# All low weight parts on VectorE, and other counts of filler products, in a two-layer mixer and MoE kernel

## The chip, the cores and the metric

One core of a Trainium2 chip runs the whole program. The time is device time of one execution in microseconds (us), and a kernel is given by the median of its runs. TensorE (PE in the rows) multiplies, VectorE (DVE), ScalarE (ACT) and GpSimd (POOL) work on vectors, SyncE (SP) issues the loads of the weights.

## What is computed

The reference is a decoder of two layers over 256 tokens of width 1024, all in float32:

```python
for layer in range(DEPTH):                                    # DEPTH = 2
    mix = token_mixers(h, ...)        # y = h @ w_in; three head groups; concat @ w_out
    h = layer_norm(DN_ALPHA * h + mix, ...)
    ffn = moe_ffn(h, ...)             # 16 experts of width 512, the router picks two of a token
    h = layer_norm(DN_ALPHA * h + ffn, ...)
```

In `token_mixers` the product `h @ w_in` is cut into columns for three groups. Group A is gated linear attention ("G" below), group B is causal softmax attention over the one block of 256 tokens ("M"). Group C ("S") is softmax attention over 64 keys that an indexer picks for each query: a score of every earlier key, and then the top 64 of each row. The three results side by side are multiplied by `w_out`.

## The kernel before

**Products.** The mixer's weights are used in two parts. `Pieces.fill` (L586) takes a piece of a weight tile `wf` that a load has brought in, lets ScalarE copy it to a rounded high part `whi` and subtracts to get the low part `wlo`; the activations are split alike (`hhi`, `hlo`). A projection then adds three products for every piece and token tile: `pj<-whi,hhi`, `pj<-whi,hlo` and `pj<-wlo,hhi`. `Pieces.next` makes some pieces ahead of their use (four in the projections, three in the output projection). Which engine subtracts is decided by the number of the piece:

```python
(pool if self.i % SHARE == SHARE - 1 and self.i >= FROM else eng).tensor_sub(lo, src, hi.bitcast(F32))
```

With SHARE 5 and FROM 24 that is GpSimd for 13 of a layer's 88 pieces. Two more are made on GpSimd at the border of the layers, by another call.

**The order of the work.** A planner, class `Order` (L78), writes one list of instructions for each engine. It keeps a clock for each engine from its own costs. A backbone makes the seven projections in the order I, V, GV, M, S, GK, GG and then the output projection. Around it run tasks (indexer, attention, linear attention), and each goes on when what it waits for is due by the planner's clock of PE. So a change of a planned cost, or of the engine of an instruction, moves the places at which the tasks' products stand between those of the backbone. In the indexer each of the eight rounds of the top-k search waits for the planner's DVE clock:

```python
for _ in range(8):
    yield lambda: od.clk["DVE"] <= od.clk["PE"] + 400
    dve.max(out=m8, in_=acc)
    dve.match_replace(out=acc, in_to_replace=m8, in_values=acc, imm_value=SENT)
```

**Attention S.** `softmax_pv` (L613) goes over two query tiles, t = 0 with 128 keys and t = 1 with 256. PE multiplies (`sc<-qkT`), DVE adds the mask of the picked keys and takes the row maxima (`s_sb,mx<-sc,acc`, four heads), ACT takes the exponentials (`s_sb<-s_sb,mx`), DVE divides (`ri`, then `s_sb<-s_sb,ri`), PE transposes (`pT<-ident,s_sb`) and multiplies by the values (`pv<-pT,v`), and ACT and DVE split the result into two `mx` tiles, called `mixS`. Group A ends in a like chain: PE `o<-W,X`, ACT squares (`sq<-o`), DVE sums them (`ms<-sq`), GpSimd takes the root (`ms<-ms,mhalf`), DVE scales and gates (`og<-o,ms`, `og<-og,sg`), PE transposes (`tr<-ident,og`), and this becomes `mixG`.

**Output projection.** It uses its eight row blocks in the order `OUT_ORDER = (4, 6, 2, 0)`, two at a time. The first two (4, 5) take group B's result, the next two (6, 7) take `mixS`, and before these the backbone waits (`yield mixS`, L1164); the last four take `mixG`. Each pair of blocks is eight groups of three products (`po<-whi,mx` x2, `po<-wlo,mx`).

**Filler.** `warm(n, w)` issues products whose result nobody reads: at the start on a tile of ones, while the first weights are loaded, and in some pauses on the identity. In the router (`choose`, L1296) the picks of each token tile (`hot`) are counted with a product `pos<-hot,strict`, DVE makes positions and selection matrices `G` from it, and PE gathers the expert's tokens with them (`xT<-G,h`).

Of the kernel before, what the change touches and what calls it, by code (L numbers as in the profile page):

```python
# [9 lines left out]
F32 = mybir.dt.float32  # L10
# [34 lines left out]
N_T4 = 9  # L45
N_SM = 10
N_WS = 4
SHARE = 5
FROM = 24
N_WO = 3  # L50
N_UNITS = ((1, 3), (2, 6))
N_WARM0 = 7
N_AHEAD = 5
LAG = 350.0
TRIG = 5487.999999999999
N_FILL = 2
N_LAST = 2
N_WARM = 2
N_LEAD = 7
N_WARM2 = 4  # L60
TWO = (1, 3, 5)
AGAIN = {(0, 'g', 5), (1, 'g', 2), (1, 'g', 0), (1, 'd', 1), (1, 'd', 6), (1, 'd', 4), (2, 'g', 3), (2, 'd', 6)}
FILL = (1, 2)
# [180 lines left out]
def trunk_kernel(ctx, tc, x, positions, w_in, gate_up, gate_bias, norm_gain, w_out, ln_mix_g, ln_mix_b,  # L244
# [8 lines left out]
    pe, act, dve, pool = od.pe, od.act, od.dve, od.pool  # L253
# [4 lines left out]
    def bank(name="ps"):  # L258
        b = pp.tile([P, 512], F32, name=name, tag="ps")
        od.take(b.tensor.name)  # L260
        return b

    def t2(name, shape=(P, 512), dt=F32):
        return wp.tile(list(shape), dt, name=name, tag="t2", bufs=N_T2)
# [80 lines left out]
    def more(n=1):  # L345
        for _ in range(n):
            while issued[0] < len(specs) and specs[issued[0]][0] in extra:
                issued[0] += 1
            if issued[0] >= len(specs):
                return  # L350
            key, (parts, nk, w) = specs[issued[0]]
            issued[0] += 1
            t = fp.tile([P, nk, w], F32, name="wf", tag="wf")
            for at, src in parts:
                nc.sync.dma_start(t[:, at[0], at[1]] if at else t.rearrange("p k n -> p (k n)"), src)
            feed[key] = t
# [66 lines left out]
    ident = cp.tile([P, P], F32, name="ident")  # L423
# [77 lines left out]
    def mm(o, a, b, start=True, stop=True):  # L501
        pe.matmul(o, a, b, start=start, stop=stop, skip_group_check=True)
# [59 lines left out]
    def warm(n, w):  # L562

        b_ = bank("warm")
        for i in range(2 * n):
            mm(b_[:, 0:P], w, ones)
        od.free(b_)

# [8 lines left out]
    class Pieces:  # L577
# [8 lines left out]
        def fill(self, eng=dve):  # L586
            while self.i < len(self.plan) and self.i < self.j + self.ahead:
                key, kk, c0, n = self.plan[self.i]
                src = feed[key][:, kk, c0:c0 + n]
                hi = t2("whi", (P, n), F32R)  # L590
                lo = t2("wlo", (P, n), F32R)
                act.activation(hi, src, AF.Copy)
                (pool if self.i % SHARE == SHARE - 1 and self.i >= FROM else eng).tensor_sub(lo, src, hi.bitcast(F32))
                units[key] = feed[key]
                self.made[self.i] = hi, lo
                self.left[key] -= 1
                if not self.left[key]:
                    feed.pop(key)
                    more()
                self.i += 1  # L600
# [72 lines left out]
    def weight_pieces(l):  # L673
        plan = []
        for key in ORDER:
            _, groups, cols = CHUNKS[key]
            for i, nk in enumerate(groups):
                plan += [((l, key, i), kk, cols[0] * j, n) for kk in range(nk) for j, n in enumerate(cols)]
        for k0 in OUT_ORDER:
            plan += [((l, "O", k0 + kk), 0, 512 * n, 512) for kk in range(2) for n in range(2)]  # L680
        return Pieces(plan, N_WS)
# [75 lines left out]

    units, begun = {}, set()
    warm(N_WARM0, ones)
    pieces = weight_pieces(0)  # L760
    hhi, hlo = halves(0)
# [4 lines left out]
    for l in range(DEPTH):  # L766
# [529 lines left out]
        def choose(t):  # L1296

            s, g = slice(t * E, t * E + E), slice(4 * t, 4 * t + 4)
            top1, top2 = (top[:, i:i + 1] for i in (2 * t, 2 * t + 1))
            x4 = sel[:, s].rearrange("p (g e) -> p g e", e=4)  # L1300
            xa, xj = (x4[:, :, :, None].to_broadcast([P, 4, 4, 4]), x4[:, :, None, :].to_broadcast([P, 4, 4, 4]))
            rank4 = rank[:, s].rearrange("p (g e) -> p g e", e=4)
            yield dve.tensor_add(sel[:, s], sc[:, s], rb)
            dve.tensor_add(sums[:, g, 0:2], x4[:, :, 0:2], x4[:, :, 2:4])
            dve.tensor_add(sums[:, g, 2:4], x4[:, :, 0::2], x4[:, :, 1::2])
            rev = bass.AP(tensor=sel.tensor, offset=sel.offset + t * E + 3, ap=[sel.ap[0], [4, 4], [-1, 2]])
            yield dve.tensor_add(sums[:, g, 4:6], x4[:, :, 0:2], rev)
            dve.tensor_reduce(gs[:, g], sums[:, g], AX.X, OP.max)
            yield dve.tensor_tensor(gt[:, g], xj, xa, op=OP.is_gt)
            dve.tensor_reduce(top1, gs[:, g], AX.X, OP.max)  # L1310
            yield dve.tensor_tensor(ge[:, g], xj, xa, op=OP.is_ge)
            dve.scalar_tensor_tensor(at[:, g], gs[:, g], top1, pref[:, 0:4], op0=OP.is_equal, op1=OP.mult)
            yield dve.copy_predicated(gt[:, g], below[:, None].to_broadcast([P, 4, 4, 4]), ge[:, g])
            dve.tensor_reduce(top2, at[:, g], AX.X, OP.max)
            yield dve.tensor_reduce(rank4, gt[:, g], AX.X, OP.add)
            yield dve.tensor_scalar(at[:, g], at[:, g], top2, None, op0=OP.is_ge)
            yield dve.scalar_tensor_tensor(hot[:, s].rearrange("p (g e) -> p g e", e=4), rank4, 1.5,
                                           at[:, g, None].to_broadcast([P, 4, 4]), op0=OP.is_lt, op1=OP.mult)
            if t == 0:
                mm(pc[:, 0:E], strict, hot[:, 0:E])  # L1320
            else:
                mm(pc[:, E:2 * E], strict, hot[:, E:2 * E])
            yield dve.tensor_scalar(pos[:, s], hot[:, s], -1000.0, 1000.0, op0=OP.mult, op1=OP.add)
            yield dve.tensor_add(pos[:, s], pos[:, s], pc[:, s])
# [159 lines left out]

        pc = bank("pos")
        steps = [choose(t) for t in range(NT)]
        for _ in range(N_LEAD):
            next(steps[0])
        score(1)
        dve.tensor_scalar(mvs[1][:, 4:5], mvs[1][:, 0:1], mvs[1][:, 3:4], -1.0, op0=OP.mult, op1=OP.mult)  # L1490
        act.activation(h[1], h[1], AF.Identity, scale=mvs[1][:, 3:4], bias=mvs[1][:, 4:5])
        warm(N_WARM, ident)
        for _ in steps[0]:
            next(steps[1])
# [68 lines left out]
        for p in range(E // 2):  # L1563
# [54 lines left out]
            for i in range(8):  # L1618
                n, k = (i // 4, i % 4) if p >= FIN - 1 else (i % 2, i // 2)
# [39 lines left out]
        if last:  # L1659
            finish(z, sb, sts, *vecs[2:])  # L1660
            break
        warm(N_WARM2, ident)

        def close(t, z, st, hhi, hlo, nxt=l + 1, sb=sb, g2=vecs[2], b2=vecs[3]):
# [56 lines left out]
```

## Time and profile before

| | before |
|---|---|
| median of 3 runs (lowest, highest) | 717.87 us (717.22, 718.0) |
| the profiled execution, its span | 717.56 us, 715.5 us |
| PE busy | 687.1 us, 96% |
| DVE busy | 443.9 us, 62% |
| ACT busy | 273.6 us, 38% |
| POOL busy | 75.0 us, 10% |
| mean granted clock of TensorE | 0.993 |
| HBM traffic, mean | 341 GB/s |

The span reaches from the first to the last instruction. The profiled execution is 2.06 us longer than its span, and lies within the three timed runs. Busy shares are means over stages that differ: a mixer of about 150 us and an expert stage of about 200 us in each layer.

### The profile page before, as it was taken

To read this page: it belongs to the slowest core of one execution; us is meant where nothing else is said; L and a number is where in the kernel's file an instruction comes from. 1 tells how busy PE (TensorE), PEld (TensorE's weight loads), DVE (VectorE), ACT (ScalarE), POOL (GpSimd) and SP (SyncE) were. 2 spreads that over 40 slices of the span, in tenths; PEclk is the share of its full clock that TensorE was granted. 3 is DMA by queue.
4 is the path that set the end of the run, shared out by engine and by line. 5 is a ranking of instruction groups with operands and counts; after the bars stand their busy time and mean duration, and the time that the engine had idled before them with its cause. 6 is when DMAs were issued, how large, how long until landed. Compare 5 with 4: busy or idle time off the path is not lost. (4 is left out here: it accounts for less than half of the span.)

```text
span 715.5 us, 11300 instructions
## 1 busy us (share of the span) xinstructions
PE 687.1 (96%) x3885; PEld 399.2 (56%) x3885; DVE 443.9 (62%) x1091; ACT 273.6 (38%) x579; POOL 75.0 (10%) x102
## 2 busy tenths in 40 slices
PE   9999999999999989999899999999999999899993
PEld 8887878843533533533487879787435334343330
DVE  6778887652445454767487787867243556259646
ACT  5578675431212201212276676564223022022121
POOL 2021022200000001200121111121000000021002
PEclk9999999999999999999999999999999999999997
DMA  9799937979999999999999844479899999999971
GB/s 306 272 388 407 408 120 250 325 293 408 409 403 408 407 407 408 408 410 407 334 391 401 313 154 146 132 251 338 323 408 408 403 407 409 407 407 409 409 288 59
DMA packets 83533, 244.05 MB, mean 341 GB/s; under 512 B 10180, under 2 KB 14344, under 8 KB 83464
## 3 DMA queue, kind: packets, MB, share of 16 engines
q1 hardware_dynamic: 82792, 242.91, 89.0%
q8 instruction: 34, 0.56, 0.3%
q10 hardware_dynamic: 416, 0.26, 0.1%
q14 instruction: 35, 0.29, 0.1%
q0 software_dynamic: 256, 0.03, 0.0%
HBM read 242.13 MB, written 1.05 MB: 340 GB/s over the span
## 5 line engine op out<-in xcount | busy, mean ns | idle before, releaser
L239 PE MATMUL gu<-wf,xT 128*64 128x512 f32 x912 | 226.0, 594 | 3.6 <-PEq L1437 3.6
L239 DVE SCALAR_TENSOR_TENSOR yt<-y,ws,yt 32x512 fp32r<-32x512 f32 (+1 forms) x116 | 86.7, 748 | 94.9 <-ACT yt L239 93.4
L239 PEld LDWEIGHTS gu<-wf,xT 128*64 128x64 f32 x912 | 71.8, 137 | 131.7 <-issue 123.3
L239 DVE TENSOR_TENSOR wlo<-wf,whi 128x512 fp32r<-128x512 f32 (+3 forms) x148 | 89.6, 640 | 39.5 <-ACT whi L239 28.5
L239 PE MATMUL y<-wf,actT 128*64 128x512 f32 x432 | 110.5, 595 | 1.8 <-ACT actT L239 1.8
L239 ACT ACTIVATE whi<-wf 128x512 fp32r<-128x512 f32 (+3 forms) x176 | 86.1, 553 | 9.8 <-PE po L239 3.6
L239 PE MATMUL pj<-whi,hhi 128*128 128x512 f32 (+2 forms) x224 | 77.4, 356 | 0.4 <-ACT whi L239 0.4
L239 ACT ACTIVATE yt<-y,ws 128x512 fp32r<-128x512 f32 x60 | 36.8, 687 | 104.5 <-PE y L239 94.9
L239 PE MATMUL pj<-whi,hlo 128*128 128x512 f32 (+2 forms) x224 | 75.4, 347 | 0.0
L239 PEld LDWEIGHTS y<-wf,actT 128*64 128x64 f32 x432 | 34.0, 137 | 54.1 <-issue 42.0
L239 DVE TENSOR_TENSOR act<-act,gu 128x512 f32<-128x512 f32 x16 | 11.0, 688 | 83.7 <-PE gu L239 77.1
L239 PE MATMUL pj<-wlo,hhi 128*128 128x512 f32 (+2 forms) x224 | 60.5, 356 | 0.4 <-DVE wlo L239 0.4
L239 POOL TENSOR_TENSOR wlo<-wf,whi 128x512 fp32r<-128x512 f32 (+3 forms) x28 | 32.4, 1158 | 220.1 <-ACT whi L239 183.6
L239 PE MATMUL gu<-wx,xT 128*64 128x512 f32 x112 | 52.7, 596 | 0.0
L239 PEld LDWEIGHTS pj<-whi,hhi 128*128 128x128 f32 x224 | 42.1, 188 | 7.3 <-issue 1.7
L239 PEld LDWEIGHTS pj<-whi,hlo 128*128 128x128 f32 x224 | 42.1, 188 | 4.7
L239 ACT ACTIVATE actT<-aT 128x512 f32<-128x512 f32 x16 | 9.5, 594 | 85.4 <-PE aT L239 85.4
L239 PEld LDWEIGHTS pj<-wlo,hhi 128*128 128x128 f32 x224 | 37.5, 188 | 6.6 <-issue 1.2
L239 ACT ACTIVATE xT<-xT,cols 128x256 f32<-128x256 f32 x32 | 17.4, 564 | 57.2 <-PE xT L239 57.2
L239 ACT ACTIVATE act<-gu 128x512 f32<-128x512 f32 x16 | 9.6, 597 | 75.9 <-PE gu L239 75.9
L239 PE MATMUL y<-wx,actT 128*64 128x512 f32 x80 | 33.4, 595 | 0.0
L239 DVE TENSOR_TENSOR z<-z,sc 128x512 f32<-128x512 f32 x48 | 29.7, 680 | 0.4 <-PE sc L239 0.4
(268 smaller groups left out, 948.1 us busy)
## 6 DMA issues: line engine op xcount, KB each, us to landing
wf<-in_w_expert_gate_dram SPq DMA_DIRECT2D x114, 512.0 KB, 10.2
wf<-in_w_expert_up_dram SPq DMA_DIRECT2D x114, 512.0 KB, 10.1
wf<-in_w_expert_down_dram SPq DMA_DIRECT2D x108, 512.0 KB, 10.0
wf<-in_w_in_dram SPq DMA_DIRECT2D x32, 512.0 KB, 9.8
wx<-in_w_expert_down_dram SPq DMA_DIRECT2D x36, 256.0 KB, 5.9
wf<-in_w_out_dram SPq DMA_DIRECT2D x16, 512.0 KB, 11.1
wx<-in_w_expert_up_dram SPq DMA_DIRECT2D x24, 256.0 KB, 6.9
wx<-in_w_expert_gate_dram SPq DMA_DIRECT2D x10, 512.0 KB, 10.1
```

Of the source, the lines that this page charges most:

```text
L239: return fn(*a, **kw)
```

## The change

All low parts that the mixer's `fill` hands out by number go to VectorE. `warm(n, w)` now issues n products where it issued 2n; two of its calls, which issued 4 and 8 products, still do, and the one at the start issues 11 where it issued 14. In `choose` two products on the identity follow the first `pos<-hot,strict`.

```diff
--- before.py
+++ after.py
@@ -45,19 +45,18 @@
 N_T4 = 9
 N_SM = 10
 N_WS = 4
-SHARE = 5
-FROM = 24
 N_WO = 3
 N_UNITS = ((1, 3), (2, 6))
-N_WARM0 = 7
+N_WARM0 = 11
+N_KEEP = 2
 N_AHEAD = 5
 LAG = 350.0
 TRIG = 5487.999999999999
 N_FILL = 2
 N_LAST = 2
-N_WARM = 2
+N_WARM = 4
 N_LEAD = 7
-N_WARM2 = 4
+N_WARM2 = 8
 TWO = (1, 3, 5)
 AGAIN = {(0, 'g', 5), (1, 'g', 2), (1, 'g', 0), (1, 'd', 1), (1, 'd', 6), (1, 'd', 4), (2, 'g', 3), (2, 'd', 6)}
 FILL = (1, 2)
@@ -562,7 +561,7 @@
     def warm(n, w):
 
         b_ = bank("warm")
-        for i in range(2 * n):
+        for i in range(n):
             mm(b_[:, 0:P], w, ones)
         od.free(b_)
 
@@ -590,7 +589,7 @@
                 hi = t2("whi", (P, n), F32R)
                 lo = t2("wlo", (P, n), F32R)
                 act.activation(hi, src, AF.Copy)
-                (pool if self.i % SHARE == SHARE - 1 and self.i >= FROM else eng).tensor_sub(lo, src, hi.bitcast(F32))
+                eng.tensor_sub(lo, src, hi.bitcast(F32))
                 units[key] = feed[key]
                 self.made[self.i] = hi, lo
                 self.left[key] -= 1
@@ -1318,6 +1317,7 @@
                                            at[:, g, None].to_broadcast([P, 4, 4]), op0=OP.is_lt, op1=OP.mult)
             if t == 0:
                 mm(pc[:, 0:E], strict, hot[:, 0:E])
+                warm(N_KEEP, ident)
             else:
                 mm(pc[:, E:2 * E], strict, hot[:, E:2 * E])
             yield dve.tensor_scalar(pos[:, s], hot[:, s], -1000.0, 1000.0, op0=OP.mult, op1=OP.add)
```

The first place that moves is attention S of t = 1 in layer 0, on PE; layer 1 moves alike. Before, the stretch of the GG projection in which its second half stands reads as below; its `sc<-qkT 128x256 x4` stands sixteen rows higher, in the same projection, and `o<-W,X` belongs to group A.

```order
L239 MATMUL o<-W,X 64x128 x8
L239 MATMUL pj<-whi,hhi 128x512
L239 MATMUL pj<-whi,hlo 128x512
L239 MATMUL pj<-whi,hhi 128x512
L239 MATMUL pj<-whi,hlo 128x512
L239 MATMUL pj<-wlo,hhi 128x512 x2
L239 MATMUL pT<-ident,s_sb 128x128 x8
L239 MATMUL pv<-pT,v 64x128 x12
```

After, the same steps stand in the output projection. Four groups of `po` stand ahead of these rows, and behind them come `tr<-ident,og 128x128 x8` and then the first `po` that uses `mixS`:

```order
L238 MATMUL sc<-qkT 128x256 x4
L238 MATMUL o<-W,X 64x128 x8
L238 MATMUL po<-whi,mx 128x512 x2
L238 MATMUL po<-wlo,mx 128x512
L238 MATMUL po<-whi,mx 128x512 x2
L238 MATMUL po<-wlo,mx 128x512
L238 MATMUL po<-whi,mx 128x512 x2
L238 MATMUL po<-wlo,mx 128x512
L238 MATMUL po<-whi,mx 128x512 x2
L238 MATMUL po<-wlo,mx 128x512
L238 MATMUL pT<-ident,s_sb 128x128 x8
L238 MATMUL pv<-pT,v 64x128 x12
```

So the scores, the transposes and the product with the values have moved from among the products of GG to between the first eight groups of the output projection, and only four groups are left between `sc` and `pT`; all `tr<-ident,og` of group A now stand behind `pv` and ahead of the other `po`.

The second place is DVE, from the last row maximum of these four heads to the division. Before:

```order
L239 ISA s_sb,mx<-sc,acc 128x256
L239 ISA mx 128x1
L239 TENSOR_SCALAR mx<-mx 128x4
L239 TENSOR_TENSOR wlo<-wf,whi 128x512
L239 SCALAR_TENSOR_TENSOR W<-W,eb,kv 64x128 x4
L239 TENSOR_TENSOR wlo<-wf,whi 128x512
L239 RECIPROCAL ri<-mx 128x4
L239 TENSOR_SCALAR s_sb<-s_sb,ri 128x256 x4
L239 SCALAR_TENSOR_TENSOR W<-W,eb,kv 64x128 x4
```

After:

```order
L238 ISA s_sb,mx<-sc,acc 128x256
L238 ISA mx 128x1
L238 TENSOR_SCALAR mx<-mx 128x4
L238 TENSOR_TENSOR wlo<-wf,whi 128x512 x2
L238 RECIPROCAL ri<-mx 128x4
L238 TENSOR_SCALAR s_sb<-s_sb,ri 128x256 x4
L238 TENSOR_REDUCE ms<-sq 128x4
L238 TENSOR_SCALAR ms<-ms 128x4
L238 TENSOR_TENSOR og<-o,ms 128x512
L238 TENSOR_TENSOR og<-og,sg 128x512 x2
```

Two `wlo` stand between the maxima and the division in both, the second of them in wait for a `whi`; after the change the whole tail of group A (`ms`, `og`) stands behind the division.

The third place is ACT around the exponentials of these heads. Before:

```order
L239 ACTIVATE s_sb,mx<-s_sb,mx 128x256 x4
L239 ACTIVATE whi<-wf 128x512 x2
L239 ACTIVATE sq<-o 128x512
L239 ACTIVATE pT<-pT 128x512 x2
L239 ACTIVATE whi<-wf 128x512
L239 ACTIVATE mx<-pv 128x512
L239 ACTIVATE sq<-o 128x512
```

After:

```order
L238 ACTIVATE whi<-wf 128x512 x2
L238 ACT_TABLE_LOAD
L238 ACTIVATE s_sb,mx<-s_sb,mx 128x256 x4
L238 ACTIVATE sq<-o 128x512
L238 ACTIVATE whi<-wf 128x512
L238 ACTIVATE pT<-pT 128x512 x2
L238 ACTIVATE mx<-pv 128x512
```

Ahead of the exponentials a load of the function table has come in, since the two `sg` of GG now run before them; behind them a squaring and one `whi` stand before the copies of the transposed tiles.

## Rows read from the trace of the kernel before

**Rows 1.** Page, parts 1 and 2: busy us of each engine; HBM traffic by slice.
```profile
PE 687.1 (96%) x3885; PEld 399.2 (56%) x3885; DVE 443.9 (62%) x1091; ACT 273.6 (38%) x579; POOL 75.0 (10%) x102
...
GB/s 306 272 388 407 408 120 250 325 293 408 409 403 408 407 407 408 408 410 407 334 391 401 313 154 146 132 251 338 323 408 408 403 407 409 407 407 409 409 288 59
```

**Rows 2.** Timeline, 101 to 115 us, layer 0: start, length, engine, operation, [wait].
```profile
101.75 1.13 PE L239 MATMUL sc<-qkT 64*128 64x256 f32 x8
...
104.43 0.63 DVE L239 TENSOR_SCALAR mx<-mx 128x4 f32<-128x4 f32 x1
...
105.10 0.51 ACT L239 ACTIVATE s_sb<-s_sb,mx 128x256 f32<-128x256 f32 x1
...
107.09 1.13 ACT L239 ACTIVATE whi<-wf 128x512 fp32r<-128x512 f32 x2
...
107.73 0.69 DVE L239 TENSOR_TENSOR wlo<-wf,whi 128x512 fp32r<-128x512 f32 x1 [0.92 <-ACT whi L239]
...
108.40 1.09 PE L239 MATMUL o<-W,X 128*64 128x128 f32 x16
...
108.55 1.15 DVE L239 TENSOR_SCALAR s_sb<-s_sb,ri 128x256 f32<-128x256 f32 x4
...
110.92 1.03 PE L239 MATMUL pT<-ident,s_sb 128*128 128x128 f32 x8
...
111.89 1.58 PE L239 MATMUL pv<-pT,v 128*64 128x128 f32 x24
112.34 0.17 DVE L239 TENSOR_SCALAR ms<-ms 128x4 f32<-128x4 f32 x1
...
112.59 1.05 POOL L239 TENSOR_TENSOR ms<-ms,mhalf 128x4 f32<-128x4 f32 x1 [7.55 <-DVE ms L239]
...
114.74 0.68 DVE L239 TENSOR_TENSOR og<-o,ms 128x512 f32<-128x512 f32 x1
```

**Rows 3.** Timeline, 117 to 123 us, layer 0, output projection.
```profile
117.11 1.28 ACT L239 ACT_TABLE_LOAD   x1
...
117.51 0.62 PE L239 MATMUL po<-whi,mx 128*128 128x512 f32 x2
...
122.28 0.61 PE L239 MATMUL po<-whi,mx 128*128 128x512 f32 x2
```

**Rows 4.** Page, part 5: the low parts made on GpSimd.
```profile
L239 POOL TENSOR_TENSOR wlo<-wf,whi 128x512 fp32r<-128x512 f32 (+3 forms) x28 | 32.4, 1158 | 220.1 <-ACT whi L239 183.6
```

**Rows 5.** Timeline, 68.9 to 70.5 us, layer 0.
```profile
68.97 1.28 POOL L239 TENSOR_TENSOR wlo<-wf,whi 128x512 fp32r<-128x512 f32 x1 [6.45 <-ACT whi L239]
69.09 1.31 DVE L239 TENSOR_TENSOR y<-rope 128x128 f32<-128x128 f32 x1
...
70.46 0.66 PE L239 MATMUL tr<-ident,y 128*128 128x128 f32 x4 [0.75 <-DVE y L239]
```

**Rows 6.** Timeline, 414 to 417 us, layer 1.
```profile
414.15 1.63 POOL L239 TENSOR_TENSOR wlo<-wf,whi 128x512 fp32r<-128x512 f32 x1 [6.07 <-ACT whi L239]
...
417.07 0.57 PE L239 MATMUL bT<-mc,la 128*128 128x128 f32 x3 [0.59 <-DVE la L239]
```

**Rows 7.** Windows of the `warm` products alone: stretch, length, PE busy (records), ...
```profile
3.00:5.00 2.00, 2.00 (x11) 2.00 (x11) 0.00 (x0) 1.00 0.80 171
...
6.25:6.75 0.50, 0.50 (x6) 0.49 (x4) 0.00 (x0) 1.00 1.05 411
```

**Rows 8.** Timeline, 5 to 7 us: the first weight piece and the first projection.
```profile
5.50 0.78 ACT L239 ACTIVATE whi<-wf 128x292 fp32r<-128x292 f32 x2 [2.94 <-DMA wf<-in_w_in_dram]
...
6.76 1.15 PE L239 MATMUL pj<-wf,hT 128*128 128x292 f32 x4
```

**Rows 9.** Timeline, router of layer 0.
```profile
147.24 1.18 PE L239 MATMUL xT<-G,h 128*128 128x128 f32 x8 [1.08 <-DVE top L239]
```

**Rows 10.** Timeline, PE alone, around 258 us: a wait in the expert stage.
```profile
258.19 1.08 PE L239 MATMUL gu<-wf,xT 128*64 128x512 f32 x4 [1.80 <-PEq L1437]
```

**Rows 11.** Windows, end of the span: PE, PEld, DVE, ACT, POOL busy; granted clock; DMA.
```profile
706.00:707.00 1.00, 0.00 (x0) 0.00 (x0) 0.96 (x4) 0.48 (x1) 0.55 (x2) 0.51 0.00 0
```

## The prediction

> **What bounds the kernel now.** The page comes first. PE is busy for 96% of the span, and no other engine is above 62% [rows 1]. The row of HBM traffic shows some 408 GB/s through the expert stages, and 120 to 340 in slices 6 to 9 and 23 to 29, where the later parts of the mixers lie [rows 1]. There neither DVE nor the memory is at its limit, so time is lost or won only where a product on PE waits for another engine, and a microsecond that PE loses in a mixer moves all that comes after. I therefore read the timeline of the mixers, looking for PE rows with a wait, and for the steps that the change puts elsewhere.
>
> **The change part by part.**
>
> *Attention S moves into the output projection.* This carries the sum. Before, its second tile (t = 1) lies in the GG projection, and from the start of `sc` at 101.75 to the start of `pT` at 110.92 PE has other products to do; its `pT` row shows no wait at all [rows 2]. After, the listing of PE leaves between `sc` and `pT` only `o<-W,X` and four groups of `po`. I price both sides from one origin, T = start of `sc`.
>
> PE's side: `sc` 1.13, `o<-W,X` 1.09 [rows 2]; seven groups of `po` lie between 117.51 and 122.28, that is 0.68 each, four make 2.73 [rows 3]. PE is through at about T+4.9.
>
> The chain's side, with the lengths that the same steps have before [rows 2]: the exponentials start at T+3.35 (105.10) and end at T+5.34 (107.09, where ACT goes on). Behind them ACT now does `sq` and one `whi`, 0.57 each (1.13 for two), until T+6.5. DVE's second `wlo` waits for that `whi`; from its start to the start of the division there were 0.82 (107.73 to 108.55), so the division starts at T+7.4, a quarter of its 1.15 is one head, and the first transposes can start at T+7.7. PE has then waited **2.8**. The last head is divided at T+8.5, so the eight transposes, which take 0.97 by themselves (110.92 to 111.89), end at T+8.8, and `pv` ends at T+10.3, 1.5 later. Meanwhile the tail of group A stands behind the division on DVE: the sum of squares, priced as the other DVE pass over 512 columns at 0.68, the scaling with its hop to GpSimd 0.25 (112.34 to 112.59), GpSimd's root 1.05, `og<-o,ms` 0.68, and the first gating another 0.68: T+8.5 plus 3.35 makes T+11.85. `tr<-ident,og` stands ahead of every further `po`, so PE waits again from T+10.3, **1.55**, and some 0.3 more for the last transposed heads and for the second half of `og`. That is 4.65. Against it the exponentials may start up to 0.45 sooner, since the scaling of the maxima took 0.63 before (104.43), and a DVE operation of the same form (112.34) 0.17. I take **4.5 us per layer, 9.0 in all**. Bounds: 3.2, if the `sq`, `whi` and `wlo` ahead of the division (0.57, 0.57 and 0.69, some 1.3 of which then falls away) find room while the scores are made; 5.7, if DVE comes to the maxima late by one wait for GpSimd's root (1.05), which now lies in the same stretch.
>
> The other edit there, one more load of a function table on ACT ahead of the exponentials, is 1.28 [rows 3]. From the end of GG ACT has two `sg`, one `pT`, two `whi` at some 0.57 each and this load, 4.1 in all, while PE does four groups (2.7) and four transposes (some 0.5) and the maxima come 3.35 after that, at 6.5. So I cost it at nothing; with that cover gone it would be 1.28 per layer. The four transposes of t = 0 come after two groups of `po`, and I cost them at nothing too, between 0 and 1.
>
> *Low parts on DVE.* GpSimd loses 26 of its 28 pieces of 1.16 [rows 4], and DVE gets 26 at 0.69 [rows 2], 18 us over both mixers. PE uses a piece in six products, two groups or 1.36, and pieces are made four ahead, so 0.69 of DVE for each is covered. What the trace shows of the other direction: beside a GpSimd piece that ran from 68.97 for 1.28, a DVE operation on 128 columns took 1.31, more than the 0.68 of one on 512, and PE waited 0.75 for it [rows 5]. In layer 1 a piece from 414.15 for 1.63 lies ahead of a wait of 0.59 [rows 6]. These two waits should go: **-1.35**, between -0.6 (one of them is refilled by the added subtractions) and -2.0 (with small ones of 0.2 elsewhere).
>
> *The start.* Three products fewer are six records. They come at about 0.2 each early on, and at 0.1 or a little less in the last half microsecond [rows 7]. The first projection starts at 6.76, right behind the filler, although its weights were there by 5.50, when ACT began to round them [rows 8]. It could start 1.0 sooner. It then lies in part in the stretch in which products still take twice as long, which gives back some 0.25, and later weights have to be there as well. I take **-0.6**, between 0 and -1.0.
>
> *The router.* The two added products are four records, at 0.1 some 0.4. They stand where PE waits 1.08 for DVE [rows 9], so they cost nothing; without that wait they would cost 0.4 per layer.
>
> *The clock.* PE's pauses in the output projection are longer than the longest that I find amid work before, 1.80, behind which the matrix products go on at their usual rate [rows 10]. At the end of the span, where PE has no more to do, the granted clock is seen at 0.51, the lower of the levels 1.2 and 2.4 GHz [rows 11]. If it fell in the new pauses, products would go at half speed for a while. If all eight groups behind the stall did, that would be 8 x 0.68 = 5.4 more per layer; I take half, 2.5, as the price, and leave it out of the sum, since the row of 1.80 is nearer to the pauses of 2.8 and 1.55 than the idle end is.
>
> The Trainium skill has a rule on this, in "TensorE: Matmul & The Clock Gate", section "HAM oscillation — how this bites in real kernels": short bursts of products with waits between them can send the clock back to its lower level at every wait. By it each layer would pay 2.5 and the sum would come to about 730; no row of this trace shows such a fall amid work.
>
> **The sum.** 9.0 - 1.35 - 0.6 = +7.05. The profiled execution took 717.56 and would take 724.6. It lies 0.3 under the median of 717.87, so I say **724.9**.
>
> **Rivals.**
> - *The clock falls in the stall.* For it: two pauses close together in each layer, with short products between. Against: 1.80 without a fall [rows 10]. It would give 727.4 with one fall and 729.9 with two.
> - *The stall is taken back, and the kernel is faster.* Its place is the expert stage: if PE there waited for weights, a mixer that ends later would find more of them landed, and only the gains would be left, 717.87 - 1.95 = 715.9. For it speaks the traffic of 408 GB/s there [rows 1]. Against it: PE is at 96%, and the one longer wait in it that I show is PE's own sequencer, not a load [rows 10]. It decides if the stall that is left in a layer is under 1.0.
> - *The change does next to nothing.* The chain is shorter than I make it, because ACT and DVE have the `whi` and `wlo` done in gaps, and PE's waits of some 1 us per layer meet the gains: 717 to 719. For it: two links (`sq`, and the second `wlo`) hang on ACT's place in its queue, and earlier ones could start sooner. Against: even without them 3.2 are left.
>
> **Chances.** The forecast, with its bounds of the stall, 0.55; a fall of the clock on top, 0.28; the stall is smaller than its bound but still outweighs the gains, 0.04; next to nothing, 0.05; the gains alone, 0.08. About 0.2%, or 1.4 us, is what a measurement of this kernel can tell from no change. So faster 0.08, same 0.05, slower 0.87. The forecast's own range is 721.3 (3.2 per layer, gains of 3.0) to 728.7 (5.7 per layer, gains of 0.6). For 8 in 10 the range has to take in most of the clock's cases: 719.5 to 731.
>
> **What the profile after would show.** If I am right: in both layers a wait of 2 to 3 us ahead of `pT<-ident,s_sb` and one of 1 to 2 ahead of `tr<-ident,og`, both ended by DVE, in the output projection; the division of `s_sb` some 7 us behind the start of its `sc`; the row `y<-rope` back at a fraction of 1.31 and no wait ahead of `tr<-ident,y` at 70; the first projection at about 5.8; `pos` to `xT` as long as before; expert stages as long as before, only later. A second granted level in the windows of the output projection would show the first rival; expert stages that are shorter by the stall the second; waits of under 1 us in the output projection the third. The prediction would be wrong above all if ACT or DVE reach the maxima and the exponentials at other times than their places in the queues suggest, since nothing in the trace of before shows these steps in this stage.

## The result, and the profile after

The changed kernel takes 723.39 us (median of 7 runs, 722.49 to 724.98), the kernel before 717.87. The ratio is 1.0074, with a 95% interval of 1.0058 to 1.0089: slower by 5.5 us. The forecast was 724.9, between 719.5 and 731.

The page after, with the busy times, the granted clock by slice and the group of low parts on DVE:

```profile
PE 691.0 (96%) x3887; PEld 401.5 (56%) x3887; DVE 443.7 (61%) x1117; ACT 276.4 (38%) x581; POOL 44.6 (6%) x76
...
PEclk9999999999999999999999999999999999999997
...
L238 DVE TENSOR_TENSOR wlo<-wf,whi 128x512 fp32r<-128x512 f32 (+3 forms) x174 | 97.2, 598 | 54.5 <-ACT whi L238 51.1
```

PE's share is as before, and DVE's busy time has not grown (443.7 us after, 443.9 before) although it makes 26 low parts more: the mean of one has fallen from 640 to 598 ns, and a DVE operation beside a GpSimd piece had been longer too [rows 5]. The slices of the clock show nothing; a finer cut will.

The timeline of the output projection in layer 0, where the forecast put its stall. First the start and the length, then the engine and the operation, and in brackets what the engine waited for:

```profile
114.13 1.13 PE L238 MATMUL sc<-qkT 64*128 64x256 f32 x8
...
117.01 0.51 ACT L238 ACTIVATE s_sb<-s_sb,mx 128x256 f32<-128x256 f32 x1 [1.24 <-DVE mx L238]
...
118.86 0.39 PE L238 MATMUL po<-wlo,mx 128*128 128x512 f32 x1
...
119.47 0.62 ACT L238 ACTIVATE whi<-wf 128x512 fp32r<-128x512 f32 x1
120.12 0.69 DVE L238 TENSOR_TENSOR wlo<-wf,whi 128x512 fp32r<-128x512 f32 x1 [2.55 <-ACT whi L238]
...
120.94 1.14 DVE L238 TENSOR_SCALAR s_sb<-s_sb,ri 128x256 f32<-128x256 f32 x4
...
121.34 1.58 PE L238 MATMUL pT<-ident,s_sb 128*128 128x128 f32 x8 [2.09 <-DVE s_sb L238]
...
122.86 2.77 PE L238 MATMUL pv<-pT,v 128*64 128x128 f32 x24
...
123.02 1.01 POOL L238 TENSOR_TENSOR ms<-ms,mhalf 128x4 f32<-128x4 f32 x1 [9.85 <-DVE ms L238]
...
124.67 1.28 DVE L238 TENSOR_TENSOR og<-og,sg 128x512 f32<-128x512 f32 x2
...
125.56 1.17 PE L238 MATMUL tr<-ident,og 128*128 128x128 f32 x8
...
126.48 1.06 PE L238 MATMUL po<-whi,mx 128*128 128x512 f32 x2
```

With T = 114.13, the start of the scores, the chain reads as follows, with the forecast behind each step. The exponentials start at T+2.9 (3.35, at most 0.45 sooner). The `whi` behind them ends at T+6.0 (6.5), the division starts at T+6.8 (7.4), the first transposes at T+7.2 (7.7). PE had its last product at T+4.7, free at about T+5.0 (4.9). So **PE waits 2.25**; the bracket of 2.09 names DVE's `s_sb` as what ended it. `tr<-ident,og` starts at T+11.4 (11.85). But the second wait of 1.55 is not there. In its place `pv` takes 2.70 from its start to the next row, where it took 1.51 before [rows 2].

The windows after show why. The columns are stretch, length, busy time of PE, PEld, DVE, ACT and POOL, then the granted clock:

```profile
119.00:121.00 2.00, 0.25 (x2) 0.00 (x0) 0.84 (x3) 1.09 (x3) 0.00 (x0) 1.00 0.00 0
121.00:123.00 2.00, 1.66 (x10) 1.17 (x12) 1.84 (x6) 0.63 (x2) 0.00 (x0) 0.74 0.52 170
123.00:125.00 2.00, 2.00 (x20) 2.00 (x22) 0.93 (x2) 0.56 (x1) 1.01 (x1) 0.50 0.23 92
125.00:127.00 2.00, 1.96 (x17) 1.33 (x13) 1.65 (x4) 1.33 (x3) 0.00 (x0) 0.90 0.00 0
...
477.00:479.00 2.00, 2.00 (x14) 1.61 (x14) 1.05 (x4) 1.20 (x2) 0.77 (x1) 0.50 0.76 262
```

The clock falls to its lower level in the stretch from 121 to 123, with the transposes behind PE's wait, and is back between 125 and 127. The same happens in layer 1 at 477. `tr<-ident,og` then waits for `og` no longer, since `pv` comes that late.

To put a price on each stage I read when PE starts it. The first is the kernel before: `po` with `mxG` in layer 0, the first projection of layer 1, `po`, and `po` with `mxG` in layer 1 (the others are in [rows 3] and [rows 8]):

```profile
129.33 0.62 PE L239 MATMUL po<-whi,mxG 128*128 128x512 f32 x2
...
356.69 1.15 PE L239 MATMUL pj<-wf,hT 128*128 128x292 f32 x4
...
468.44 0.62 PE L239 MATMUL po<-whi,mx 128*128 128x512 f32 x2
...
481.50 0.62 PE L239 MATMUL po<-whi,mxG 128*128 128x512 f32 x2
```

The kernel after, the first `po` of layer 0 first:

```profile
110.83 0.62 PE L238 MATMUL po<-whi,mx 128*128 128x512 f32 x2
...
132.40 0.39 PE L238 MATMUL po<-whi,mxG 128*128 128x512 f32 x1
...
359.83 0.41 PE L238 MATMUL pj<-wf,hT 128*128 128x292 f32 x1
...
466.04 0.62 PE L238 MATMUL po<-whi,mx 128*128 128x512 f32 x2
...
487.56 0.62 PE L238 MATMUL po<-whi,mxG 128*128 128x512 f32 x2
```

Between the first `po` and the first that uses `mxG` lay 11.82 us in layer 0 and 13.06 in layer 1; now there are 21.57 and 21.52. By the starts of the rows the products that moved in take 0.35 (`pT` of t = 0) + 1.06 + 1.03 + 0.97 + 1.51 = 4.92 in layer 0, and 3.9 in layer 1, where one `o<-W,X` of 1.02 stood in the output projection before. What is left is the stall: **4.8 and 4.6, or 9.4**. From the first projection to the first `po` there were 110.75 and 111.75; now, with the moved work added again, there are 109.84 and 110.11, that is 0.9 and 1.6 less. Nothing else moves: the expert stage of layer 0 and the border of the layers take 227.4 both times (129.33 to 356.69, 132.40 to 359.83).

The start, after, with the first four of the first projection's 32 products:

```profile
5.91 1.16 PE L238 MATMUL pj<-wf,hT 128*128 128x292 f32 x4
...
14.13 0.51 PE L238 MATMUL pj<-whi,hhi 128*128 128x292 f32 x1
```

and the second of these rows in the kernel before:

```profile
14.42 0.51 PE L239 MATMUL pj<-whi,hhi 128*128 128x292 f32 x1
```

The first projection starts 0.85 sooner (5.91, and 6.76 in [rows 8]), as its filler is over, but when it comes to its split products only 0.29 is left. So 0.56 of the start is given back within the first projection. None of it goes to a lower rate, since the first four products take 1.16, and 1.15 in the kernel before [rows 8]. It goes to gaps: the products start 0.25 apart, but the fifth and sixth 0.53 and 0.35 behind their neighbours, and the 25th and 26th 0.32 and 0.35, 0.55 more in all. The 0.9 of layer 0 is **1.5** without these 0.56; with the 1.6 of layer 1 the mixers' projections have gained **3.1**. The sum 9.4 - 3.1 - 0.3 = 6.0 is what the first `po` with `mxG` of layer 1 has moved by (481.50 to 487.56). In the router the row behind the two added products shows the wait left over, 0.53, and the step from `pos` to `xT` takes 149.04 to 150.29, 1.25, as before:

```profile
150.29 1.18 PE L238 MATMUL xT<-G,h 128*128 128x128 f32 x8 [0.53 <-DVE top L238]
```

### The profile page after: what moved, and what is told of

It reads as the page before. It is cut to its first block, busy times and chain, and to the rows that moved or that the text cites. A ratio compares the mean times of both kernels' runs of the same rounds, so it can differ in the third digit from the quotient of the medians.

```text
span 721.7 us, 11299 instructions
## 1 busy us (share of the span) xinstructions
PE 691.0 (96%) x3887; PEld 401.5 (56%) x3887; DVE 443.7 (61%) x1117; ACT 276.4 (38%) x581; POOL 44.6 (6%) x76
## 5 line engine op out<-in xcount | busy, mean ns | idle before, releaser
L238 DVE TENSOR_TENSOR wlo<-wf,whi 128x512 fp32r<-128x512 f32 (+3 forms) x174 | 97.2, 598 | 54.5 <-ACT whi L238 51.1
L238 PE MATMUL sc<-yt,sT 128*128 128x512 f32 x72 | 23.8, 430 | 1.7 <-ACT yt L238 1.6
```

Source lines behind the costliest of these rows:

```text
L238: return fn(*a, **kw)
```

## The experiments

Two theories. **Order:** the loss is the place of attention S in the output projection, and low parts on DVE cost nothing. **Load:** DVE's added work delays the chains wherever they stand. Each kernel was timed in five rounds beside the kernel before; the ratios are to that.

**1. The filler alone.** The changed kernel, sharing with GpSimd again; the planner gives the order of before.

```diff
-                eng.tensor_sub(lo, src, hi.bitcast(F32))
+                (pool if self.i % 5 == 4 and self.i >= 24 else eng).tensor_sub(lo, src, hi.bitcast(F32))
```

> The changed kernel with the low parts shared with GpSimd again, so only the filler products differ from before: 11 products at the start, two in the router's pause. The planner gives the order of before. Both theories expect the gain of the start alone, about -0.9 us (717.0): the first projection began 0.86 us sooner in the profile after. A rival on the router: if the two added products are not covered by PE's wait there, they give 0.4 us back in each layer, and the time is 717.8, as before.

Measured: 717.35 against 717.89, ratio 0.9990 (0.9981 to 0.9999). The gain is 0.5, not 0.9, and may be less: 9 of the 27 executions of the kernel before had a lower mean granted clock (0.989 or 0.991) and took 718.5 or more, none of this run's 11 did, and the median of the other 18 is 717.58. The rival on the router is out by the row above, where 0.53 of PE's wait is left. PE alone at the start of this run:

```profile
5.63 1.19 PE L238 MATMUL pj<-wf,hT 128*128 128x292 f32 x4
6.98 0.76 PE L238 MATMUL pj<-wf,hT 128*128 128x292 f32 x2 [0.15 <-DMA wf<-in_w_in_dram]
```

The fifth product of the projection waits for a weight load. The first four take 1.19, nearly the 1.15 of before [rows 8]. So it is the weights that take part of the gain back.

**2. The low parts alone.** The kernel before, and only the sharing taken away.

```diff
-                (pool if self.i % SHARE == SHARE - 1 and self.i >= FROM else eng).tensor_sub(lo, src, hi.bitcast(F32))
+                eng.tensor_sub(lo, src, hi.bitcast(F32))
```

> The kernel before with all low parts handed out by number on DVE, and nothing else. The planner gives the order of the changed kernel. Theory (the order costs the time): the stall of about 4.6 us per layer less the waits that GpSimd made, so 717.9 + 9.2 - 2.3 = 724.8, with 723.5 to 725 allowed for the clock. Rival (the filler at the start, through another phase of the clock, has a part in the loss): 718 to 721.

Measured: 723.31, ratio 1.0066 (1.0052 to 1.0080). The loss is this edit's, and the rival on the filler is out. It is 1.5 less than I expected, and not longer than the changed kernel (723.39), so in this order no gain of the filler is seen.

**3. DVE's work in the order of before.** A second lane issues on VectorE but is planned as GpSimd.

```diff
+    ghost = _Lane(od, nc.vector, "POOL")
...
-                eng.tensor_sub(lo, src, hi.bitcast(F32))
+                (ghost if self.i % 5 == 4 and self.i >= 24 else eng).tensor_sub(lo, src, hi.bitcast(F32))
```

> The changed kernel, with all low parts on DVE, but planned as if every fifth still went to GpSimd. So the products on PE stand in the order of before, and DVE does the 18 us more. Theory (the order costs the time, the engine costs nothing): the gains alone, 717.9 - 0.9 - 2.3 = 714.7. Rival (DVE's added work delays the chains wherever they stand): no better than the changed kernel with its stall halved, 719 or more. If DVE's work and the absence of GpSimd's cancel: 717.0.

Measured: 717.90, ratio 0.9999 (0.9990 to 1.0008). The stall of 9.4 is gone with the order, so far the order theory holds. But its other half, that the engine costs nothing, falls: the expected 714.7 is missed by 3.2. The waits for GpSimd's neighbours [rows 5, 6] are gone, and two others have come, in PE's rows:

```profile
81.19 0.82 PE L238 MATMUL pT<-ident,s_sb 128*128 128x128 f32 x4 [0.80 <-DVE s_sb L238]
...
435.42 0.63 PE L238 MATMUL tr<-ident,y 128*128 128x128 f32 x4 [1.07 <-DVE y L238]
```

DVE ahead of the first of them:

```profile
78.63 0.69 DVE L238 TENSOR_TENSOR wlo<-wf,whi 128x512 fp32r<-128x512 f32 x1 [1.42 <-ACT whi L238]
...
79.95 0.29 DVE L238 MAX8 m<-acc 128x8 f32<-128x128 f32 x1
...
80.75 0.87 DVE L238 TENSOR_SCALAR s_sb<-s_sb,ri 128x128 f32<-128x128 f32 x4
```

DVE stands idle for 1.42 until the `whi` of the added `wlo` is there, does the subtraction, then rounds of the top-k search until 80.6, and only then the division for attention M that PE wants; beside the filler-only run it is 1.2 behind there. At 430.5 in layer 1 an added `wlo` waits for 0.71 in the same way. So what costs time is not DVE's load as such, but a subtraction whose input is late and which holds up what stands behind it in DVE's list. Its place there comes from a plan in which GpSimd does it.

**4. Earlier top-k rounds.** The changed kernel, with DVE allowed further ahead in the planner.

```diff
-                    yield lambda: od.clk["DVE"] <= od.clk["PE"] + 400
+                    yield lambda: od.clk["DVE"] <= od.clk["PE"] + 1200
```

> The changed kernel with one number more: the rounds of the top-k search may go on while the planner's DVE clock is up to 1200 ns ahead of its PE clock, where it was 400. The planner then places the scores of t = 1 before the GG projection ends and ahead of its place in before, and the transposes and values inside GG. Theory (order): no stall in the output projection, 714 to 716. Rival (DVE's load): the top-k rounds of t = 0, planned more tightly, hold up DVE, PE waits for low parts or scores elsewhere, and the time stays at 720 or more.

Measured: 719.05, ratio 1.0013 (1.0002 to 1.0024). It lies between the two: the stall is gone (13.06 from the first `po` to the first with `mxG` in both layers), and another wait of PE has come in layer 0, ahead of the gate's product, with a fall of the clock behind it:

```profile
52.02 1.10 PE L238 MATMUL gx<-mc,rT 17*128 17x256 f32 x4 [1.34 <-issue]
```

```profile
54.00:56.00 2.00, 2.00 (x7) 1.52 (x6) 1.86 (x6) 1.95 (x4) 0.00 (x0) 0.50 1.02 408
```

Up to the first `mxG` layer 0 takes 2.1 longer than in experiment 1.

**5. One link out of the chain.** The order of the changed kernel, with piece 77, whose `wlo` stands ahead of the division, subtracted by GpSimd.

```diff
+    ghost = _Lane(od, nc.gpsimd, "DVE")
...
-                eng.tensor_sub(lo, src, hi.bitcast(F32))
+                (ghost if self.i == 77 else eng).tensor_sub(lo, src, hi.bitcast(F32))
```

> The changed kernel with its order, but the low part of piece 77, the one that stands between the exponentials and the division of t = 1 and waits for a whi behind them, is subtracted by GpSimd in both layers. Theory (the stall is this chain, link by link): the division no longer waits for squaring, whi and wlo; it starts some 1.6 us sooner behind its scores (about 5.2 instead of 6.8), PE's wait ahead of pT falls from 2.25 to 0.7, the tail of group A moves up with it, and the time falls by 1.5 per layer to 720.4. Rival (the stall belongs to the place of the products, and what stands between on DVE is not its price; or GpSimd's piece holds DVE and the root up for as long): 722.5 to 723.4.

Measured: 720.72, ratio 1.0047 (1.0033 to 1.0061), against 1.0074 for the changed kernel. That is 3.3 over the kernel before in its batch (717.38), where the changed kernel is 5.5 over it in its own, so 2.2 are saved and not the 3.0 that were expected; that the time itself comes out near 720.4 is in part the batch. Its division, its `pT`, GpSimd's piece, and `tr` of `og`:

```profile
119.13 1.14 DVE L238 TENSOR_SCALAR s_sb<-s_sb,ri 128x256 f32<-128x256 f32 x4
...
119.54 1.23 PE L238 MATMUL pT<-ident,s_sb 128*128 128x128 f32 x8 [0.49 <-DVE s_sb L238]
119.96 1.44 POOL L238 TENSOR_TENSOR wlo<-wf,whi 128x512 fp32r<-128x512 f32 x1 [7.01 <-ACT whi L238]
...
124.00 1.23 PE L238 MATMUL tr<-ident,og 128*128 128x128 f32 x8 [1.72 <-DVE og L238]
```

The scores start at 113.92, so the division starts at T+5.2, to the digit, and PE's wait ahead of `pT` is down to 0.65 (0.49 in the bracket). The clock stays at its upper level in the output projection, and there the second wait is: 1.72 ahead of `tr<-ident,og`. From the first `po` to the first with `mxG` it takes 19.92 and 19.93, 1.6 less per layer than the changed kernel, as expected. What is missing from the 3.0 lies elsewhere: in this execution the clock fell in layer 1's projections, which took 1.3 longer. So the stall is the chain that I had added up, link by link.

**6. The clock held up.** The changed kernel with products that nobody reads in both pauses.

```diff
+N_HOLD = (10, 6)
...
                 b_ = bank("pT")
+                if (v0, t, h0) == (256, 1, 0):
+                    for _ in range(N_HOLD[0]):
+                        nc.tensor.matmul(b_[:, 0:P], ident, ones, start=True, stop=True, skip_group_check=True)
...
                 b_ = bank("tr")
+                if t == 0:
+                    for _ in range(N_HOLD[1]):
+                        nc.tensor.matmul(b_[:, 0:P], ident, ones, start=True, stop=True, skip_group_check=True)
```

> The changed kernel with products that nobody reads put into its two pauses on PE: ten ahead of pT (2.2 us) and six ahead of tr of og (1.3 us), in both layers, so that PE hardly pauses. The granted clock should then stay at 1.00 in the windows of the output projection, where the profile after shows 0.5. Theory (the lower clock there is mostly covered, since the tail of group A on DVE and GpSimd ends last anyway): 0.3 to 0.6 us less per layer, 722.4 to 722.8. Rival (the lower clock is a large part of the loss): 1.5 or more less per layer, 720.4. If the fillers run beyond the pauses: 724.

Measured: 723.40, ratio 1.0079 (1.0066 to 1.0092). The windows of the output projection in layer 0:

```profile
119.00:121.00 2.00, 2.00 (x20) 1.97 (x18) 1.16 (x4) 0.77 (x2) 0.00 (x0) 1.00 0.00 0
121.00:123.00 2.00, 2.00 (x24) 1.62 (x24) 1.53 (x5) 1.09 (x2) 0.29 (x1) 1.00 0.73 231
123.00:125.00 2.00, 2.00 (x26) 1.83 (x22) 1.25 (x3) 0.60 (x1) 0.72 (x1) 1.00 0.08 31
```

The clock holds, in layer 1 too. From the first `po` to the first with `mxG` it takes 21.21 and 21.24, 0.3 less per layer than the changed kernel (21.57 and 21.52). So the lower clock costs 0.3 per layer there, not the 2.5 of my rival: what runs at half speed lies beside the tail of group A, which ends last in any case. The whole time did not fall by the 0.6, so the expected 722.4 to 722.8 was missed, and the profile has one reason: in this execution the clock fell in another place, in layer 1's projections, where the changed kernel has 1.00 throughout, and these took 1.3 longer:

```profile
410.00:412.00 2.00, 2.00 (x6) 1.52 (x6) 1.86 (x7) 1.97 (x3) 0.00 (x0) 0.50 0.68 207
```

The clock fell at the same place in the profiled execution of experiment 5. The single times fit the small price. Of the five executions here those at a mean granted clock of 0.993 and 0.994 took 722.56 and 722.20, the others 723.40 to 724.20. Of the seven of the changed kernel the two at 0.993 took 722.69 and 722.49, the others, at 0.989 or 0.986, 723.36 or more. That those two had no fall in the output projection is not shown, as only the profiled execution has a trace.

**7. Two pieces to DVE.** The first experiment's kernel, and two pieces more on DVE.

```diff
+    ghost = _Lane(od, nc.vector, "POOL")
...
+                (ghost if (key[0], self.i) in ((0, 54), (1, 49)) else pool if self.i % 5 == 4 and self.i >= 24 else eng).tensor_sub(lo, src, hi.bitcast(F32))
```

> The order of before, with 11 products at the start and two in the router's pause, and all of GpSimd's pieces left with GpSimd but two: piece 54 of layer 0 and piece 49 of layer 1, beside which DVE operations were held and PE waited 0.91 and 0.74 in the profile of before. Theory (each such wait is one GpSimd piece beside one DVE operation that PE waits for; DVE has room for one piece): both waits go, 717.4 - 1.6 = 715.8. Rival (DVE has no room there, so the wait comes back behind the added subtraction, as in the run with the order of before): 717 or more.

Measured: 716.17, ratio 0.9983 (0.9975 to 0.9992). That is 1.2 under the kernel before in its batch, where the start (0.5) and the two waits (1.6) should give 2.1. `tr<-ident,y`, which waited 0.75 [rows 5], follows its neighbour at once:

```profile
68.93 0.60 PE L238 MATMUL tr<-ident,y 128*128 128x128 f32 x4
```

**8. Less filler.** The first experiment's kernel with 8 products at the start.

```diff
-N_WARM0 = 11
+N_WARM0 = 8
```

> The order and sharing of before, two products in the router's pause, and 8 products at the start instead of 11. Theory (the start is bounded by the weights that follow the first, and by products at half rate): the first projection begins up to 0.6 sooner again, but ends within 0.3 of the kernel with 11, so 717.1 to 717.6. Rival (the filler at the start is pure loss): 716.8. If the products at half rate cost more than the start brings: 717.7 or more.

Measured: 717.36, ratio 1.0005 (0.9996 to 1.0015). The kernel before stood at 717.38 in this batch, so the gain of the 11 is not seen here. Five of its eleven executions took 718.27 to 719.22, at the same mean granted clock as the others; why is open. PE at the start waits for loads, 0.64 and 0.41:

```profile
5.48 1.22 PE L238 MATMUL pj<-wf,hT 128*128 128x292 f32 x4 [0.64 <-DMA wf<-in_w_in_dram]
7.10 1.25 PE L238 MATMUL pj<-wf,hT 128*128 128x292 f32 x4 [0.41 <-DMA wf<-in_w_in_dram]
```

**9. One piece kept on GpSimd.** The third experiment's kernel, with piece 59 left to GpSimd in both layers.

```diff
-                (ghost if self.i % 5 == 4 and self.i >= 24 else eng).tensor_sub(lo, src, hi.bitcast(F32))
+                (pool if self.i == 59 else ghost if self.i % 5 == 4 and self.i >= 24 else eng).tensor_sub(lo, src, hi.bitcast(F32))
```

> The run with the order of before and all low parts on DVE, but with piece 59 of each layer, one of the GK projection's, left with GpSimd as the planner has it. In that run PE waited 0.95 us at 80 us and 1.23 at 434 behind DVE's top-k rounds, a place where before GpSimd did this piece. Theory (DVE has no room for one more subtraction in that stretch, and room elsewhere): both waits go and the time falls from 717.9 to 715.7. Rival (DVE is late there from all pieces ahead of it, so one piece back frees 0.69 at each place at most): 716.6 to 717.2. If DVE's load is not the cause: 717.9.

Measured: 715.68 against 717.97, ratio 0.9969 (0.9957 to 0.9980). It is faster than both kernels, and 2.3 us faster than the one before. PE's row at 80 us has no wait:

```profile
80.23 0.81 PE L238 MATMUL pT<-ident,s_sb 128*128 128x128 f32 x4
```

The wait at 434 is gone too. Twelve of a layer's thirteen pieces can go to DVE; the thirteenth of each layer cost 2.2 in both layers together, more by the waits for its `whi` in experiment 3 (1.42 and 0.71) than by its subtraction (0.69).

**10. Attention S back in GG.** As the fourth experiment, with 1000.

```diff
-                    yield lambda: od.clk["DVE"] <= od.clk["PE"] + 400
+                    yield lambda: od.clk["DVE"] <= od.clk["PE"] + 1000
```

> The changed kernel with the number in the top-k search at 1000 instead of 400. All low parts are on DVE, and the planner puts the scores, transposes and values of t = 1 back among the products of GG, with some 35 rows between scores and transposes. Theory (the stall of 9.2 us in the changed kernel is the place of attention S in the output projection): no wait over 0.5 ahead of pT or tr of og there, and with what DVE's load costs in the denser stretch (2.2 in the order of before) 715 to 718.5. Rival (with all pieces on DVE the loss only moves, into the top-k stretch): 720 or more.

Measured: 722.49, ratio 1.0064 (1.0047 to 1.0082). I missed this by 4. The output projection did as expected: no wait ahead of `pT` or `tr` of `og`, and 13.1 us to the first `mxG` in both layers. But the rival came true in layer 0, in another place. Three rows of PE there, and the windows over them:

```profile
51.18 0.50 PE L238 MATMUL pj<-whi,hhi 128*128 128x512 f32 x1 [0.90 <-ACT W L238]
...
54.29 0.79 PE L238 MATMUL rw<-mc,ones 128*128 128x128 f32 x2 [1.02 <-DVE mc L238]
...
56.16 0.63 PE L238 MATMUL pj<-whi,hhi 128*128 128x512 f32 x1
```

```profile
52.00:54.00 2.00, 1.26 (x4) 0.56 (x4) 0.66 (x2) 1.98 (x5) 0.00 (x0) 0.67 1.05 405
54.00:56.00 2.00, 1.71 (x6) 1.62 (x7) 1.86 (x8) 1.97 (x3) 0.00 (x0) 0.50 1.04 416
```

PE waits for ACT's `W`, the clock falls between 52 and 54, PE waits for DVE's `mc`, and the products behind that go at half rate. In the profile the first `po` with `mxG` of layer 0 starts at 132.47, 3.6 behind that of experiment 1 (128.83), and layer 1 adds 0.6. I take it that the planner has put tasks together there that stood apart; which of them is to blame was not tried. The profiled execution took 721.11. Of the six, three took 720.37 to 721.17 at a mean granted clock of 0.990 to 0.992, and three 723.82 to 724.12 at 0.984, so the median lies between two groups, and where the second lost 3 us more is not shown.

## Why the prediction was right, and where its steps were not

**The bound** was read rightly: time was lost where PE waits in a mixer, and passed on to the end (6.0 at the last landmark, 6.2 in the span). The rival by which the expert stage takes the stall back is out, with 227.4 us both times.

**Attention S in the output projection.** The forecast was 4.5 per layer, 9.0 in all; the profile has 9.4. The chain is right in its links (experiment 5 takes one out, and the output projection shortens by the 1.6 expected) and in its cause (the changed kernel and experiment 3 do the same work on the same engines in another order, and lie 5.5 apart). With the clock held up, in experiment 6, the same subtraction of stages leaves 4.5 and 4.3, so the forecast, which had no fall of the clock in it, holds there too. The division started 0.6 sooner than added up: the exponentials did by 0.47, about the bound that I gave, and the steps that I listed (6.5 and 0.82) make 7.3, not 7.4.

**The clock** fell, in both layers of the profiled execution, where I had left it out of the sum. The mechanism of the rival was there and its price was not: 0.3 per layer by experiment 6, where I had priced 2.5. I had priced the groups behind the stall at half speed. But the half speed fell mostly on `pv`, in time in which PE would otherwise have waited for `og`, and only the first `po` behind it was slow. The rule of "TensorE: Matmul & The Clock Gate" in the Trainium skill, on waits between short bursts in its section "HAM oscillation — how this bites in real kernels", said that it can fall at such waits: the windows after agree with it, with 0.50. The clock did not fall at every wait, though: in experiment 5 it stayed up over 0.65 and 1.72 in the same place. The 730 that I worked out beside it was wrong by the price.

**Low parts on DVE.** The forecast was -1.35, with -2.0 as its bound, and the profile has -3.1. The sign was right, and the reason incomplete. The engine alone brings less than 3.1: experiment 9 keeps the order of before, has twelve of the thirteen pieces on DVE without new waits, and gains 1.75 over experiment 1 by the medians, each against the kernel before in its batch, and 1.3 in the projections of the profiles. That is within my bound. The other 1.3 to 1.8 came only with the changed order; the wait of 0.39 for a `whi` in layer 1 (at 412.6 in the trace of before) is one part of it, and the rest was not taken apart. My sum had no term for what the new order does in the projections. I took the added subtractions to be covered everywhere, because pieces are made four ahead. Experiment 3 shows that they are not: in the order of before they cost PE some 2.2 in waits in the GK stretch, a little more than the 1.6 that GpSimd's absence brings, and it ends 0.55 behind experiment 1. What I left out is that DVE goes through its list in order, so a subtraction that waits for its `whi` (1.42 in experiment 3) holds up the division and the top-k rounds behind it, whatever the slack of the piece itself. In the changed kernel the planner counted the subtractions on DVE and put the rounds off: the last round of layer 0 starts at 99.60, at 84.53 before and at 84.21 in experiment 3, and attention S came to stand in the output projection. Experiments 4 and 10 let the rounds come sooner, and it is back in GG. That the gain of the projections comes from the same shift is likely, but not shown.

**The start.** The forecast was -0.6, the profile has -0.3, and experiment 1 between -0.2 and -0.5; experiments 2 and 8 show no gain of the filler. I named two things that take it back. The lower rate took nothing (1.16 for the first four products, 1.15 before). What took the 0.56 are the gaps in the projection, and for the first of them experiment 1 names a later weight. **The router** cost nothing, as forecast. **The added table load** was hidden, as forecast: it ends ahead of the exponentials, which wait for DVE's maxima.

The sum was mis-sized in its second term above all: the forecast had 9.0 - 1.35 - 0.6 = 7.05, the profile 9.4 - 3.1 - 0.3 = 6.0. The span grew by 6.2, the profiled execution by 5.8, and the medians lie 5.5 apart, so the forecast was 1.5 too high. That second term, with what the new order brought in the projections, was taken 1.75 too small; the stall and the start, 0.4 and 0.3 off, make up for some of it.

## What to carry to other kernels

Where a planner with costs writes the order, an edit that moves work to another engine also moves the order, and the second effect can be the larger: build one kernel that issues the new way and is planned the old way, and the two come apart. A chain that moves to a place with little other work is priced by adding its links against the work left beside it; that sum held to 5% here. An engine that is busy 62% on the whole can still come late in the one stretch that counts, so ask of each moved piece when its input comes and what stands behind it in its engine's list.

## What was not expected of the hardware

The clock fell after a pause of 2.25 us with held-up transposes behind it, and stayed up over pauses of 1.80 [rows 10] and 1.72 (experiment 5). The length of the pause does not decide it: the clock also fell behind a wait of 1.34 (experiment 4), and behind one of 0.94 ahead of `gx` in layer 1 in experiments 5 and 6, while the changed kernel has that wait of 0.94 too and stayed at 1.00. What decides these runs do not settle. Executions of one kernel differ as well: the kernel before took 717.45 at a mean granted clock of 0.993 and 718.84 and 718.53 at 0.991 beside experiments 1 to 4. A fall is not always a loss: it cost 0.3 where another engine ended last, and 1.3 in layer 1's projections. DVE's busy time stayed the same with 26 subtractions more; one row that shows how is the division of four heads in layer 0, 1.92 beside a GpSimd piece in experiment 1 and 0.87 without one in experiment 3.
